# Attention's product with the values in float32, four token tiles at a time

## The chip, the cores and the metric

The kernel runs on one core of a Trainium2 chip. The metric is the device time of one execution in microseconds (us); lower is better. Engine names are those of the profile: PE is TensorE's matrix multiply, PEld its weight load, DVE is VectorE, ACT is ScalarE, POOL is GpSimd, SP is SyncE, which issues the DMAs.

## The reference

One encoder layer on a sequence of 1024 tokens with 1024 channels, all in float32: half a SwiGLU step, a mixing step, half a SwiGLU step, a last RMSNorm. The mixing step projects the normed tokens once and runs two groups of eight heads, latent attention and retention; their outputs are joined and go through one output projection. The change lies in the attention group:

```python
s = (jnp.einsum('bqhd,bkhd->bhqk', qn, k_nope).astype(jnp.float32)
     + jnp.einsum('bqhr,bkr->bhqk', qp, k_pe).astype(jnp.float32))
p = jax.nn.softmax(s * MLA_SCALE, axis=-1)
return jnp.einsum('bhqk,bkhd->bqhd', p.astype(v.dtype), v)
```

There are 8 heads, 1024 queries, 1024 keys, and 64 columns of values to a head. The last line is the product that the change rewrites.

## The kernel before

The program keeps the token sequence as eight tiles of 128 tokens. Its matrix products run on operands of type FP32R (the form that the profile prints as fp32r when it is written; as a matmul operand it prints f32). Where the accuracy needs it, a float32 matrix is kept as two FP32R parts: a rounded copy, made by ACT, and the remainder, which DVE or POOL makes by subtraction. The helper `split` (lines 68 to 83, ACT at L75, subtraction at L79) does this. The helper `mm3` (L118 to L120) multiplies two such pairs with three matmuls.

The layer runs in stages: first feed-forward step, projection, retention, preparation of attention (`mla_prepare`), attention (`attention`), output projection (`out_project`), second feed-forward step, last norm.

In `mla_prepare`, the function `values(t)` forms the values of a token tile with `mm3` into the PSUM tile `dn`, and splits them into the tile `vhl`: for each token tile and head 64 columns of rounded values followed by 64 columns of remainders. A head's slice of `vhl` is thus a stationary operand of 128 keys by 128 columns.

`attention` walks over the 64 pairs of head h and token tile t, in the order h, then t. Step i issues the following:

- `scores(h, t)`: six matmuls of 512 columns (L118 to L120) into the PSUM tile `mm`, a minimum over the row on DVE (`mx`, L1486), and the exponential on ACT (`pr`, L1490), with the row sum as a side result.
- `queries` of the next head at t = 1, eight transposes; `keys2` or `keys` of another head pair at t = 3.
- `flip` of the tile before (i - 1): eight PE transposes of `pr` (L1503) in two halves, each evacuated by `split` into the tile `pT`, as rounded part (ACT) and remainder (DVE). A `pT` tile holds two token tiles, that is 256 query columns, in two parts.
- `values(h, u)` for the pair of token tiles that ended at i - 2: for each of the eight key tiles two matmuls (L1516), the rounded and the remainder part of `pT` against the same `vhl` slice. The result has 128 partitions: the product with the rounded values above, that with the remainders below. ACT copies it to SBUF (`ota`, L1519).
- `finish(h, u)` at i - 4: two transposes of that result (L1526), a DVE reduction that adds the two halves (`ona`, L1528), the reciprocal of the row sums (`ri`, L1531), and a multiplication on POOL (L1532) into the tile that the output projection reads.

The code's order is a priority and not a fixed sequence: the framework that compiles the kernel orders each engine's instructions ahead of time, the earlier-issued first, but lets a later one pass where it reckons that the earlier one's inputs aren't there yet. The PSUM tiles `mm`, `tp` and `dn` have two buffers each. Near the end of the loop, five calls of `next(after)` start parts of the output projection.

Retention, a stage earlier, has its own product with values in two versions. Even heads use two FP32R parts (L1174), with 128 stationary columns. Odd heads use plain float32 with 64 stationary columns:

```python
if whole(h):
    t = (half * 2 + c) * R2 + r
    nc.tensor.matmul(u[0:HD, c * C:(c + 1) * C],
                     self.rv[:, t, h * HD:(h + 1) * HD], shl[:, 1 - r],
```

The line L1167 that the profile names is this call; it has 256 moving columns. It is issued 32 times in the program (four odd heads, two halves, two chunks, two row tiles). Retention's `states` (L1090) is float32 too, with 64 stationary and 128 moving columns; a call issues 16 products, eight that write the lower 64 PSUM partitions and then eight that write the upper 64.

Of the kernel before, what the change touches and what calls it, by code (L numbers as in the profile page):

```python
# [12 lines left out]
F32 = mybir.dt.float32  # L13
F32R = mybir.dt.float32r
# [3 lines left out]
ALU = mybir.AluOpType  # L18
# [3 lines left out]
P = 128  # L22
S = 1024
NT = S // P
# [37 lines left out]
class Layer:  # L62
# [1281 lines left out]
    def mla_prepare(self, raw, w_uq, w_ukv):  # L1344


        nc, v, c = self.nc, self.nc.vector, self.c
        NQ = HA * QH
        raws = [raw[:, i * S:(i + 1) * S] for i in range(3)]
        nc.sync.dma_start(out=raws[0], in_=w_ukv[0])  # L1350
        for j in range(2):
            nc.sync.dma_start(out=raws[1 + j][:, 0:NQ], in_=w_uq[0][j * P:(j + 1) * P, :])
        qpool, pool = yield

        def heads(t):
            return t.rearrange("p (h d) -> p h d", h=HA)

        def transposes(col, tiles, rows=P):
            ps = self.ps.tile([P, 512], F32, name="tp")
            for j, (t, k) in enumerate(tiles):  # L1360
                nc.tensor.transpose(ps[0:rows, j * P:(j + 1) * P],
                                    c[:, t, col + k * P:col + k * P + rows], self.ident)
            return ps

        cqTs = {}

        def cq(u):
            ps = transposes(0, [(2 * u + i, j) for i in range(2) for j in range(2)])
            cqTs[u] = qpool.tile([P, 2, 2, 2, P], F32R, name="cqT")
            dst = cqTs[u].rearrange("p s i j n -> p s (i j n)")  # L1370
            self.split(ps, dst[:, 0], dst[:, 1])

        wv = pool.tile([P, 2, HA * HD], F32R, name="wv", bufs=1)
        wq = qpool.tile([P, 2, 2, NQ], F32R, name="wq", bufs=1)
        again = pool.tile([P, S], F32, name="rawm", bufs=1)
        nc.sync.dma_start(out=again, in_=w_ukv[0])
        cq(0)
        for j in range(2):
            self.split(raws[1 + j][:, 0:NQ], wq[:, 0, j], wq[:, 1, j])
        cq(1)  # L1380
        self.split(raws[0].rearrange("p (h s d) -> p h s d", h=HA, s=2)[:, :, 1],
                   heads(wv[:, 0]), heads(wv[:, 1]))
        keep, vpool = yield
        self.ckvT = keep.tile([P, 2, S], F32R, name="ckvT")
        self.wk = keep.tile([P, 2, HA * HD], F32R, name="wk")
        self.kT = [keep.tile([P, 2, S], F32R, name=f"kT{i}") for i in range(2)]
        self.vhl = vpool.tile([P, NT, HA, 2, HD], F32R, name="vhl")

        def ckv(half):
            ps = transposes(QL, [(half * 4 + j, 0) for j in range(4)])  # L1390
            hs = slice(half * 512, (half + 1) * 512)
            self.split(ps, self.ckvT[:, 0, hs], self.ckvT[:, 1, hs])

        def kpe(half):
            ps = transposes(NC0 - QH, [(half * 4 + j, 0) for j in range(4)], QH)
            hs, pe = slice(half * 512, (half + 1) * 512), slice(HD, QH)
            for kt in self.kT:
                self.split(ps[pe], kt[pe, 0, hs], kt[pe, 1, hs], scale=-SCALE)

        def queries(t):  # L1400
            cqT = cqTs[t // 2]
            q_ps = self.ps.tile([P, S], F32, name="mm")[:, 32:32 + NQ]
            for ns in (slice(0, 5 * QH), slice(5 * QH, NQ)):
                for j in range(2):
                    self.mm3(q_ps[:, ns], (cqT[:, 0, t % 2, j], cqT[:, 1, t % 2, j]),
                             (wq[:, 0, j, ns], wq[:, 1, j, ns]), j == 0, j == 1)
            src, dst = heads(q_ps), self.qn[:, t]
            nc.scalar.activation(out=dst[:, :, 0:HD], in_=src[:, :, 0:HD], func=AF.Copy,
                                 scale=-SCALE)
            self.rope(pool, src[:, :, HD:QH], dst[:, :, HD:QH],  # L1410
                      self.cos[:, t, ::2], self.sin[:, t, ::2], HA, RD // 2)

        def values(t):
            ts_ = slice(t * P, (t + 1) * P)
            v_ps = self.ps.tile([P, 512], F32, name="dn")
            self.mm3(v_ps, (self.ckvT[:, 0, ts_], self.ckvT[:, 1, ts_]),
                     (wv[:, 0], wv[:, 1]), True, True)
            self.split(heads(v_ps), self.vhl[:, t, :, 0], self.vhl[:, t, :, 1])

        ckv(0)  # L1420
        queries(0)
        ckv(1)
        queries(1)
        cq(2)
        self.split(again.rearrange("p (h s d) -> p h s d", h=HA, s=2)[:, :, 0],
                   heads(self.wk[:, 0]), heads(self.wk[:, 1]))
        for t in range(2, NT + 2):
            values(t - 2)
            if t < NT:
                queries(t)  # L1430
            if t == 3:
                cq(3)
            if t in (4, 5):
                kpe(t - 4)

    def attention(self, small, pool, after):
# [35 lines left out]
                hs = slice(half * 512, (half + 1) * 512)  # L1472
                self.split(ps[0:QH], qT[0:QH, 0, hs], qT[0:QH, 1, hs])

        sums, pts = {}, {}

        def scores(h, t):
            kT, qT = self.kT[h % 2], qTs[h]
            ts_ = slice(t * P, (t + 1) * P)
            ps = self.ps.tile([P, S], F32, name="mm")  # L1480
            for n in range(2):
                ns = slice(n * 512, (n + 1) * 512)
                self.mm3(ps[:, ns], (qT[0:QH, 0, ts_], qT[0:QH, 1, ts_]),
                         (kT[0:QH, 0, ns], kT[0:QH, 1, ns]), True, True)
            mx = small.tile([P, 1], F32, name="mx", bufs=4)
            v.tensor_reduce(out=mx, in_=ps, axis=AX.X, op=ALU.min)  # L1486
            pr = pool.tile([P, S], F32, name="pr")
            if t % 2 == 0:
                sums[h, t // 2] = small.tile([P, 2], F32, name="sum", bufs=6)
            nc.scalar.activation(out=pr, in_=ps, func=AF.Exp, scale=-1.0, bias=mx,  # L1490
                                 accum_out=sums[h, t // 2][:, t % 2:t % 2 + 1])
            pts[h, t] = pr

        def flip(h, t):
            pr = pts.pop((h, t))
            if t % 2 == 0:
                pts[h, "T", t // 2] = pool.tile([P, 2, NT, 2 * P], F32R, name="pT")
            pT = pts[h, "T", t // 2]
            for half in range(2):
                ps = self.ps.tile([P, 512], F32, name="tp")  # L1500
                for j in range(4):
                    kt = half * 4 + j
                    nc.tensor.transpose(ps[:, j * P:(j + 1) * P], pr[:, kt * P:(kt + 1) * P],  # L1503
                                        self.ident)
                k4, qs = slice(half * 4, half * 4 + 4), slice(t % 2 * P, (t % 2 + 1) * P)
                self.split(ps.rearrange("p (j q) -> p j q", j=4), pT[:, 0, k4, qs],
                           pT[:, 1, k4, qs])

        def values(h, u):
            pT = pts.pop((h, "T", u))  # L1510
            ps = self.ps.tile([P, 512], F32, name="dn")
            o = ps[:, 0:2 * P]
            for kt in range(NT):
                vl = self.vhl[:, kt, h].rearrange("p s d -> p (s d)")
                for x in range(2):
                    nc.tensor.matmul(o, vl, pT[:, x, kt], start=(kt == 0 and x == 0),  # L1516
                                     stop=(kt == NT - 1 and x == 1))
            ot = small.tile([P, 2 * P], F32, name="ota")
            nc.scalar.copy(out=ot, in_=o)  # L1519
            pts[h, "O", u] = ot  # L1520

        def finish(h, u):
            ot = pts.pop((h, "O", u))
            ps = self.ps.tile([P, 512], F32, name="dn")
            for j in range(2):
                nc.tensor.transpose(ps[:, j * P:(j + 1) * P], ot[:, j * P:(j + 1) * P], self.ident)  # L1526
            on = small.tile([P, 2, HD], F32, name="ona", bufs=1)
            v.tensor_reduce(out=on, in_=ps[:, 0:2 * P].rearrange("p (j s e) -> p j e s", j=2, s=2),  # L1528
                            axis=AX.X, op=ALU.add)
            ri = small.tile([P, 2], F32, name="ri", bufs=6)  # L1530
            v.reciprocal(out=ri, in_=sums.pop((h, u)))  # L1531
            nc.gpsimd.tensor_tensor(out=mixed[:, 2 * u:2 * u + 2, h // 2, h % 2 * HD:(h % 2 + 1) * HD], in0=on,  # L1532
                                    in1=ri.unsqueeze(2).broadcast_to([P, 2, HD]), op=ALU.mult)

        seq = [(h, t) for h in range(HA) for t in range(NT)]
        for i in range(len(seq) + 6):
# [13 lines left out]
                        keys(h // 2 + 1)  # L1550
            if 0 <= i - 1 < len(seq):
                flip(*seq[i - 1])
            for lag, fn in ((2, values), (4, finish)):
                if 0 <= i - lag < len(seq) and seq[i - lag][1] % 2 == 1:
                    fn(seq[i - lag][0], seq[i - lag][1] // 2)
            if i - len(seq) in (-6, -5, -4, -3, 0):
                next(after)

# [127 lines left out]
```

## Time and profile before

| | |
|---|---|
| median of 3 runs | 2060.51 us (2058.77 to 2062.7) |
| profiled execution, time | 2055.27 us |
| profiled execution, span of the core | 2053.1 us |
| mean granted TensorE clock | 0.993 |
| PE busy | 1978.5 us (96%), 10776 records |
| PEld busy | 1699.0 us (83%) |
| DVE busy | 1323.3 us (64%) |
| ACT busy | 818.6 us (40%) |
| POOL busy | 697.4 us (34%) |

A busy time is the union of an engine's records. PE's records overlap each other, since matmuls are pipelined and their ends are modelled; what a matmul costs on PE is therefore read from the distance between the starts of neighbouring records, and not from a record's length.

### The profile page before, as it was taken

The numbers are of one execution on the slowest core, as the hardware profiler recorded it, in microseconds if no ns is written. First come the engines' busy times: TensorE is split into PE (matmuls) and PEld (weight loads), VectorE is DVE, ScalarE is ACT, GpSimd is POOL, SyncE is SP. The second block draws the span as 40 slices with busy tenths as digits, with TensorE's granted clock in tenths as the row PEclk, the third lists the DMA queues.
The fourth block names the chain that finished last, engine by engine and source line by source line (L and its number), as shares of the span: only waits on it lengthen the run. The fifth ranks groups of instructions, "written<-read, shape, count | busy, mean of one in ns | idle before, by whom it ended". The sixth has DMA issues, their size and how long they took to land. (4 is left out here: it accounts for less than half of the span.)

```text
span 2053.1 us, 28597 instructions
## 1 busy us (share of the span) xinstructions
PE 1978.5 (96%) x10776; PEld 1699.0 (83%) x10776; DVE 1323.3 (64%) x2032; ACT 818.6 (40%) x1422; POOL 697.4 (34%) x614
## 2 busy tenths in 40 slices
PE   6999999989999999999999999999999999989998
PEld 5778888877888899998788888997788888868876
DVE  7766666655756644427878887458666566555566
ACT  5322232223444322236567776234222322324444
POOL 0255756754310013213521110000456666553112
PEclk9999999999999999999999999999999999999999
DMA  5244445457866111100100000141354454568773
GB/s 174 67 134 167 141 164 168 142 174 272 282 214 212 42 52 42 53 22 1 57 1 1 1 1 22 42 154 47 108 176 141 156 174 144 174 221 328 226 234 113
DMA packets 209338, 258.86 MB, mean 126 GB/s; under 512 B 14128, under 2 KB 126000, under 8 KB 209200
## 3 DMA queue, kind: packets, MB, share of 16 engines
q1 hardware_dynamic: 208048, 254.93, 37.4%
q8 instruction: 85, 1.39, 0.3%
q10 hardware_dynamic: 1152, 2.10, 0.3%
q14 instruction: 53, 0.43, 0.1%
HBM read 185.15 MB, written 71.83 MB: 125 GB/s over the span
## 5 line engine op out<-in xcount | busy, mean ns | idle before, releaser
L290 PE MATMUL mm<-xt,gu 128*128 128x512 f32 x1584 | 384.8, 392 | 3.3 <-DVE h L322 2.9
L290 PEld LDWEIGHTS mm<-xt,gu 128*128 128x128 f32 x1584 | 298.3, 189 | 66.2 <-ACT h L319 3.7
L79 DVE TENSOR_TENSOR gu<-s,gu 128x512 fp32r<-128x512 f32 x176 | 204.2, 1167 | 140.4 <-ACT gu L75 140.1
L79 DVE TENSOR_TENSOR wd<-rawd,wd 128x1024 fp32r<-128x1024 f32 x143 | 193.8, 1361 | 136.6 <-ACT wd L75 135.7
L290 PE MATMUL dn<-x,gu 128*128 128x512 f32 x1056 | 258.3, 392 | 1.4 <-ACT x L75 1.4
L290 PEld LDWEIGHTS dn<-x,gu 128*128 128x128 f32 x1056 | 197.3, 188 | 42.7 <-ACT x L75 2.0
L75 ACT CAST wd<-rawd 128x1024 fp32r<-128x1024 f32 x143 | 150.4, 1052 | 205.4 <-DMA rawd<-wdt 69.0
L270 POOL TENSOR_TENSOR s<-raw 128x512 f32<-128x512 f32 x40 | 53.8, 1346 | 466.9 <-DMA raw<-in_ffn_w_up 381.9
L619 PE MATMUL mm<-wd 128*128 128x512 f32 x792 | 183.0, 391 | 2.2 <-DVE wd L79 2.0
L619 PEld LDWEIGHTS mm<-wd 128*128 128x128 f32 x792 | 147.9, 188 | 36.3 <-DVE wd L79 5.7
L75 ACT CAST gu<-s 128x512 fp32r<-128x512 f32 x176 | 104.2, 618 | 164.2 <-POOL s L271 154.6
L79 DVE TENSOR_TENSOR gu<-raw,gu 128x512 fp32r<-128x512 f32 x132 | 117.5, 891 | 72.3 <-ACT gu L75 68.8
L322 DVE TENSOR_TENSOR h<-mm,h 128x512 f32<-128x512 f32 x176 | 120.8, 686 | 66.9 <-PE mm L290 66.1
L619 PE MATMUL dn<-wd 128*128 128x512 f32 x462 | 134.2, 396 | 17.6 <-ACT wd L75 13.4
L352 ACT ACTIVATE h<-h 128x512 f32<-128x512 f32 x44 | 27.8, 632 | 286.5 <-DVE h L322 286.5
L290 PE MATMUL tp<-xt,gu 128*128 128x512 f32 x528 | 128.7, 391 | 6.2 <-ACT gu L75 3.3
L619 PE MATMUL tp<-wd 128*128 128x512 f32 x462 | 130.7, 390 | 0.0
L290 PE MATMUL mm<-x,gu 128*128 128x512 f32 x528 | 127.3, 390 | 0.0
L290 PEld LDWEIGHTS tp<-xt,gu 128*128 128x128 f32 x528 | 98.4, 188 | 29.7 <-ACT gu L75 4.6
L619 PEld LDWEIGHTS dn<-wd 128*128 128x128 f32 x462 | 86.6, 189 | 39.6 <-ACT wd L75 14.3
L290 PEld LDWEIGHTS mm<-x,gu 128*128 128x128 f32 x528 | 98.8, 188 | 21.4 <-DVE h L322 0.6
L75 ACT CAST gu<-raw 128x512 fp32r<-128x512 f32 x132 | 81.1, 618 | 59.6 <-DMA raw<-in_ffn_w_gate 58.8
(356 smaller groups left out, 3881.7 us busy)
## 6 DMA issues: line engine op xcount, KB each, us to landing
hid<-h SPq DMA_DIRECT2D x154, 256.0 KB, 3.3
rawd<-hid SPq DMA_DIRECT2D x154, 256.0 KB, 3.3
raw<-in_ffn_w_gate SPq DMA_DIRECT2D x52, 512.0 KB, 4.2
raw<-in_ffn_w_up SPq DMA_DIRECT2D x44, 512.0 KB, 5.9
rawd<-wdt SPq DMA_DIRECT2D x88, 256.0 KB, 3.8
early<-in_ffn_w_down SPq DMA_DIRECT2D x40, 512.0 KB, 5.5
wdt<-early SPq DMA_DIRECT2D x80, 256.0 KB, 2.2
rawd<-in_ffn_w_down SPq DMA_DIRECT2D x66, 256.0 KB, 3.6
```

Of the source, the lines that this page charges most:

```text
L75: a = nc.scalar.copy(out=hi, in_=src)
L79: b = eng.tensor_tensor(out=lo, in0=src, in1=hi.bitcast(F32), op=ALU.subtract)
L270: tt(out=s[1], in0=u[:, h1], in1=u[:, h2], op=ALU.add)
L290: nc.tensor.matmul(out, l[:, p], r[:, q], start=start and dt == 0 and i == 0, stop=dt == 3 and i == 2, skip_group_check=True)
L322: v.tensor_tensor(out=out, in0=ps, in1=other, op=ALU.add)
L352: nc.scalar.activation(out=g, in_=g, func=AF.Silu)
L619: nc.tensor.matmul(out, w[:, p, 0, ts_], w[:, q, 1], start=start and i == 0, stop=stop and i == 2, skip_group_check=True)
```

## The change

The values stay whole: `v` is one float32 tile with 64 columns a head, written by one ACT copy, and no remainders are formed. `flip` copies the transposed probabilities whole too, one half by ACT and the other by DVE. A `pT` tile now holds four token tiles (512 query columns) in one float32 part. `values` runs one float32 matmul per key tile, 64 stationary and 512 moving columns, into the lower 64 partitions; it is issued in two parts of four matmuls, at i - 2 and i - 3. `finish` transposes four blocks of 64 partitions and multiplies straight out of PSUM on DVE; the reduction and the POOL multiplication are gone.

```diff
-        self.vhl = vpool.tile([P, NT, HA, 2, HD], F32R, name="vhl")
+        self.v = vpool.tile([P, NT, HA * HD], F32, name="v")
...
-            self.split(heads(v_ps), self.vhl[:, t, :, 0], self.vhl[:, t, :, 1])
+            nc.scalar.copy(out=self.v[:, t], in_=v_ps)
...
-        sums, pts = {}, {}
+        sums, pts, G = {}, {}, 4
...
-                pts[h, "T", t // 2] = pool.tile([P, 2, NT, 2 * P], F32R, name="pT")
+                pts[h, "T", t // G] = pool.tile([P, NT, G * P], F32, name="pT")
...
-                k4, qs = slice(half * 4, half * 4 + 4), slice(t % 2 * P, (t % 2 + 1) * P)
-                self.split(ps.rearrange("p (j q) -> p j q", j=4), pT[:, 0, k4, qs],
-                           pT[:, 1, k4, qs])
-
-        def values(h, u):
-            pT = pts.pop((h, "T", u))
-            ps = self.ps.tile([P, 512], F32, name="dn")
-            o = ps[:, 0:2 * P]
-            for kt in range(NT):
-                vl = self.vhl[:, kt, h].rearrange("p s d -> p (s d)")
-                for x in range(2):
-                    nc.tensor.matmul(o, vl, pT[:, x, kt], start=(kt == 0 and x == 0),
-                                     stop=(kt == NT - 1 and x == 1))
-            ot = small.tile([P, 2 * P], F32, name="ota")
-            nc.scalar.copy(out=ot, in_=o)
+                dst = pT[:, half * 4:half * 4 + 4, t % G * P:(t % G + 1) * P]
+                src = ps.rearrange("p (j q) -> p j q", j=4)
+                if half:
+                    v.tensor_copy(out=dst, in_=src)
+                else:
+                    nc.scalar.copy(out=dst, in_=src)
+
+        def values(h, u, part):
+
+            if part == 0:
+                pts[h, "V", u] = self.ps.tile([P, G * P], F32, name="dn")
+            pT, o = pts[h, "T", u], pts[h, "V", u][0:HD]
+            for kt in range(part * NT // 2, (part + 1) * NT // 2):
+                nc.tensor.matmul(o, self.v[:, kt, h * HD:(h + 1) * HD], pT[:, kt],
+                                 start=kt == 0, stop=kt == NT - 1)
+            if part == 0:
+                return
+            del pts[h, "T", u], pts[h, "V", u]
+            ot = small.tile([P, G * P], F32, name="ota")
+            nc.scalar.copy(out=ot[0:HD], in_=o)
             pts[h, "O", u] = ot
...
-            for j in range(2):
-                nc.tensor.transpose(ps[:, j * P:(j + 1) * P], ot[:, j * P:(j + 1) * P], self.ident)
-            on = small.tile([P, 2, HD], F32, name="ona", bufs=1)
-            v.tensor_reduce(out=on, in_=ps[:, 0:2 * P].rearrange("p (j s e) -> p j e s", j=2, s=2),
-                            axis=AX.X, op=ALU.add)
-            ri = small.tile([P, 2], F32, name="ri", bufs=6)
+            for j in range(G):
+                nc.tensor.transpose(ps[:, j * HD:(j + 1) * HD], ot[0:HD, j * P:(j + 1) * P],
+                                    self.ident[0:HD, 0:HD])
+            ri = small.tile([P, G], F32, name="ri", bufs=6)
             v.reciprocal(out=ri, in_=sums.pop((h, u)))
-            nc.gpsimd.tensor_tensor(out=mixed[:, 2 * u:2 * u + 2, h // 2, h % 2 * HD:(h % 2 + 1) * HD], in0=on,
-                                    in1=ri.unsqueeze(2).broadcast_to([P, 2, HD]), op=ALU.mult)
+            v.tensor_tensor(out=mixed[:, G * u:G * (u + 1), h // 2, h % 2 * HD:(h % 2 + 1) * HD],
+                            in0=ps[:, 0:G * HD].rearrange("p (j e) -> p j e", j=G),
+                            in1=ri.unsqueeze(2).broadcast_to([P, G, HD]), op=ALU.mult)
...
-            for lag, fn in ((2, values), (4, finish)):
-                if 0 <= i - lag < len(seq) and seq[i - lag][1] % 2 == 1:
-                    fn(seq[i - lag][0], seq[i - lag][1] // 2)
+            for lag, fn, args in ((2, values, (0,)), (3, values, (1,)), (4, finish, ())):
+                if 0 <= i - lag < len(seq) and seq[i - lag][1] % G == G - 1:
+                    fn(seq[i - lag][0], seq[i - lag][1] // G, *args)
```

## Rows read from the trace of the kernel before

**Rows 1.** Windows of the attention stage: each engine's busy us (instructions), granted clock, DMA share.

```profile
1050.00:1100.00 50.00, 49.88 (x325) 44.02 (x324) 39.58 (x58) 35.84 (x70) 2.79 (x6) 0.97 0.00 1
1100.00:1150.00 50.00, 49.85 (x340) 44.41 (x339) 41.24 (x62) 36.93 (x72) 4.54 (x9) 1.00 0.01 1
...
sum 228.00, PE 226.96 PEld 201.75 DVE 184.49 ACT 165.94 POOL 20.94; mean PE 45.39 PEld 40.35 DVE 36.90 ACT 33.19 POOL 4.19
```

**Rows 2.** Timeline of PE in attention: start, us, engine, line, operation, tiles, shapes, count.

```profile
1113.02 1.09 PE L1503 MATMUL tp<-ident,pr 128*128 128x128 f32 x8
1113.87 1.67 PE L1516 MATMUL dn<-pT,vhl 128*128 128x256 f32 x12
1115.38 0.38 PE L1526 MATMUL dn<-ident,ota 128*128 128x128 f32 x2
1115.52 0.48 PE L118 MATMUL mm<-kT,qTa 96*128 96x512 f32 x1
...
1116.99 1.04 PE L1503 MATMUL tp<-ident,pr 128*128 128x128 f32 x8
1117.78 0.47 PE L118 MATMUL mm<-kT,qTa 96*128 96x512 f32 x1
...
1119.25 0.64 PE L1516 MATMUL dn<-pT,vhl 128*128 128x256 f32 x4
1119.86 1.09 PE L1503 MATMUL tp<-ident,pr 128*128 128x128 f32 x8
...
1126.70 1.09 PE L1503 MATMUL tp<-ident,pr 128*128 128x128 f32 x8
```

**Rows 3.** Timeline of all engines, the chain of one tile's probabilities.

```profile
1117.19 1.22 DVE L1486 TENSOR_REDUCE mx<-mm 128x1 f32<-128x1024 f32 x1 [0.83 <-PE mm L120]
...
1118.59 1.13 ACT L1490 ACTIVATE pr<-mm,mx 128x1024 f32<-128x1024 f32 x1
...
1119.86 0.86 PEld L1503 LDWEIGHTS tp<-ident,pr 128*128 128x128 f32 x8 [0.18 <-ACT pr L1490]
```

**Rows 4.** Groups by form, attention stage: busy us, mean ns, idle before and its releaser.

```profile
L79 DVE TENSOR_TENSOR pT<-tp,pT 128x512 fp32r<-128x512 f32 x128 | 83.1, 684 | 15.0 <-ACT pT L75 15.0
...
L1516 PE MATMUL dn<-pT,vhl 128*128 128x256 f32 x512 | 76.2, 290 | 0.6 <-ACT pT L75 0.2
...
L75 ACT CAST pT<-tp 128x512 fp32r<-128x512 f32 x128 | 69.9, 589 | 57.4 <-PE tp L1503 56.4
...
L1528 DVE TENSOR_REDUCE ona<-dn 128x128 f32<-128x256 f32 x32 | 13.5, 421 | 6.5 <-PE dn L1526 5.7
...
L1519 ACT COPY ota<-dn 128x256 f32<-128x256 f32 x32 | 12.2, 380 | 1.4 <-PE dn L1516 1.4
```

**Rows 5.** Retention's float32 product, the line's own view: ns min/median/max.

```profile
L1167 PEld LDWEIGHTS dn<-x,rv x64: 132/137/137, 935.9 to 1012.0; 128*64 128x64 f32 x64
L1167 PE MATMUL dn<-x,rv x64: 379/379/430, 935.9 to 1012.3; 128*64 128x256 f32 x64
```

**Rows 6.** Timeline of PE around two float32 blocks in retention.

```profile
947.52 0.60 PE L1014 MATMUL tp<-ident,rk 128*128 128x128 f32 x4
948.05 1.94 PE L1167 MATMUL dn<-x,rv 128*64 128x256 f32 x8
949.92 0.38 PE L118 MATMUL mm<-x 128*128 128x256 f32 x1
...
957.79 1.94 PE L1167 MATMUL dn<-x,rv 128*64 128x256 f32 x8
959.57 0.60 PE L1090 MATMUL tp<-x,rk 128*64 128x128 f32 x4
```

**Rows 7.** Timeline of PE over retention's `states`, both partition halves.

```profile
959.57 3.28 PE L1090 MATMUL tp<-x,rk 128*64 128x128 f32 x32
962.78 0.39 PE L118 MATMUL mm<-x 128*128 128x256 f32 x1
```

**Rows 8.** The same call in the line's own view: ns min/median/max.

```profile
L1090 PE MATMUL tp<-x,rk x32: 272/272/323, 959.6 to 962.6; 128*64 128x128 f32 x32
```

**Rows 9.** Waits between 1000 and 1050 us: engine, line, what it waited for, us, times, longest.

```profile
PE dn L118 <- DVE vhl L79: 1.4, 1, 1.4
```

More of the change, by code (lines that the diff above doesn't have):

```diff
@@ L1487, in scores @@
             pr = pool.tile([P, S], F32, name="pr")
-            if t % 2 == 0:
-                sums[h, t // 2] = small.tile([P, 2], F32, name="sum", bufs=6)
+            if t % G == 0:
+                sums[h, t // G] = small.tile([P, G], F32, name="sum", bufs=6)
             nc.scalar.activation(out=pr, in_=ps, func=AF.Exp, scale=-1.0, bias=mx,
-                                 accum_out=sums[h, t // 2][:, t % 2:t % 2 + 1])
+                                 accum_out=sums[h, t // G][:, t % G:t % G + 1])
             pts[h, t] = pr
@@ L1495, in flip @@
             pr = pts.pop((h, t))
-            if t % 2 == 0:
-                pts[h, "T", t // 2] = pool.tile([P, 2, NT, 2 * P], F32R, name="pT")
-            pT = pts[h, "T", t // 2]
+            if t % G == 0:
+                pts[h, "T", t // G] = pool.tile([P, NT, G * P], F32, name="pT")
+            pT = pts[h, "T", t // G]
             for half in range(2):
```

## The prediction

> **What bounds the kernel now.** I read the page's busy shares first (PE 96%), and then the windows of the stage that the change touches, since a share over the whole span says nothing of one stage. In attention, PE is busy for 226.96 of 228 us, DVE for 184.49, ACT for 165.94 and POOL for 20.94 [rows 1]. Busy PE alone proves little, because its records overlap; so I went to the timeline, to see whether PE's starts follow each other without holes. They do. From the flip at 1113.02 to the flip at 1126.70 four token tiles pass in 13.68 us, 6.84 for a pair [rows 2], and the pair is made up of PE work alone: two flips (0.85 and 0.79), two sets of scores (1.47 each), the product with the values in two pieces (12 matmuls from 1113.87 to 1115.38 = 1.51, and 4 from 1119.25 to 1119.86 = 0.61), and two transposes of finish (0.14). The reader is to see that the only hole is inside the 0.61: four matmuls at 0.12 each take 0.48, and the flip behind them waited the rest for the exponential (0.18 by the weight load's row) [rows 3]. So PE is the bound of this stage, and what the change does to PE is what it does to the time. The pulled-forward piece of four also shows what fills such holes: the product with the values is the only work that may come early.
>
> **The product itself.** Before: 2.12 us for a pair of token tiles (1.51 + 0.61), 4.24 for four, and there are 16 groups of four (8 heads, two each), 67.8 us in all. That is 512 matmuls [rows 4].
>
> After: eight float32 products for a group, 128 in all. What is one worth? Retention has float32 products with the same 64 stationary columns and 128 partitions, and 256 moving columns. The code issues 32 of them, the trace has 64 records [rows 5]: a float32 product is two records, each with its weight load. Eight records last from 957.79 to 959.57, when a block of the same form follows: 1.78 us [rows 6]. The first record of a block can be 0.05 longer (430 against 379 ns) [rows 5], so a record comes every (1.78 - 0.05) / 8 = 0.216 us. With 128 moving columns, four records span 0.60, the last of them lasting 0.27 [rows 6, 8]: (0.60 - 0.27) / 3 = 0.11. Doubling the columns adds 0.107, so at 512 columns I expect 0.216 + 2 x 0.107 = 0.43. Sixteen records make 6.88 us for a group.
>
> The trace has another price to read there. The form with 64 stationary columns is entered and left with a gap. Four transposes at 0.109 should take 0.44, but the float32 block starts 0.53 after them (947.52 to 948.05); the same eight records take 1.87 when a 128-column form follows (948.05 to 949.92) and 1.78 when it doesn't [rows 6]. With the first record's 0.05 that is 0.09 + 0.05 + 0.09 = 0.23 for a block. Between the 128-column forms of attention I see no such gap: eight flips and the change to values take 0.85, no more than 8 x 0.109 [rows 2]. How many blocks will a group make? The two parts of `values` are issued a step apart, with a flip and scores between them, so two; and where a flip waits for its exponential, a product will be pulled forward as the four matmuls are now, which cuts the first part in two. I take three blocks: 0.70 for a group; two would be 0.46, five 1.15, none 0.
>
> So the group goes from 4.24 to 6.88 + 0.70 = 7.58, and 16 x 3.34 = **+53.4 us**.
>
> **Holes that open.** From the last score matmul's slot (1116.99) to its flip (1119.86) 2.87 us pass: the minimum (1.22), the exponential (1.13) and the hand-overs [rows 2, 3]. PE fills them with the flip before (0.79) and the next scores (1.47); 0.61 must come from elsewhere. In the new order, per four tiles, two flips have a part of `values` ahead of them (some 3.5 us each). The flip of a group's first tile can have a product pulled forward, or the eight transposes of `queries`. The flip of the last tile has only finish, four transposes, up to 0.44: 0.17 is left, 16 x 0.17 = **+2.7** (bounds 0, and 16 x 0.61 = 9.8).
>
> **Finish.** Four transposes of 128 columns for a group now (0.14 to 0.22 a pair), four of 64 partitions and 64 moving columns after. The trace has no such form. Bounds: half the price, -0.22 for a group, and the old price with one 0.19 entry and exit; -3.5 and +3.0 in all. I take **0**, since the weight load of 128 columns stays. The DVE reduction, the reciprocal count and the POOL multiplication change off the path.
>
> **DVE and ACT.** DVE loses 128 subtractions of 684 ns (87.6 us) and 32 reductions (13.5), and gets 64 copies, at most 684 each (43.8), and 16 multiplications, at most 684 each (11) [rows 4]: some 138 us left. ACT loses 64 of 128 casts of 589 (37.7); 16 copies of twice the size replace 32 of 380 ns (from 12.2 to at most 12.2): some 128 left. All of this relief is costed at nothing: PE's unbroken starts hide both engines now [rows 1, 2], and will hide them better when PE's work grows. If that cover were gone, the minimum would be what a queue on DVE delays, and the hole above would grow by the length of one copy.
>
> **Preparation.** Eight subtractions leave DVE. One of them held a PSUM buffer so that PE waited 1.4 us [rows 9]; ACT's copy stays, so I take **-1.4** (bounds 0 and -2.8, the same wait twice). `v` is 16 KB a partition smaller than `vhl`, which moves the pools that are opened after it; no row shows a wait on such memory, so 0. The change issues no DMA and moves none past another.
>
> **The sum** is 53.4 + 2.7 - 1.4 = +54.7, made against the profiled execution (2055.27, of which 2053.1 is span), which gives 2110. That execution lies 5.2 below the median of the runs shown; against the median the sum gives 2060.5 + 54.7 = **2115.2 us**.
>
> **The rivals.** *The float32 records overlap.* This is the one that ends not slower. In `states` 16 records write the lower 64 partitions, then 16 the upper; the 32 take 3.21 us up to the next form, where 32 x 0.109 + 0.09 would be 3.58 [rows 7]. About 0.37 is saved, so records of 64 columns do run at once to some extent where the two halves meet. If the new ones paired up like that, 16 records would take 3.44, the group 4.14, 16 x -0.10 = -1.6, and with +2.7 and -1.4 the time would be 2060.2; it decides from a record distance of 0.21 down. Against it: all new products write partitions 0 to 63, as retention's do, and those follow each other at the full 0.216 [rows 6].
>
> The Trainium skill, page TensorEngine Tiling (Array Packing), sections Tiling Modes and Performance Considerations, says that operands of at most 64 columns let the array run as two independent tiles, up to twice as fast, each tied to its own PSUM partitions. The overlap at the border [rows 7] agrees with it; read as a plain factor of two it would give this rival's time, read with its tie to partitions it gives none here.
>
> *No gaps, no holes.* The switches are hidden, or the parts lie in fewer blocks, and finish fills the last hole: 16 x (6.88 - 4.24) - 1.4 = +40.8, 2101. For it: longer records leave more time to load weights, 137 ns in 430 [rows 5]. Against it: they were visible with 216 [rows 6].
>
> *The flips lose their cover.* The compiled order leaves the products in one piece in each group, and three more flips of each group wait 0.61: 16 x 1.83 = +29, 2144. For it: the order was worked out ahead of time from reckoned durations, and the pieces are coarser, 0.86 each. Against it: today's order fills every hole but 0.13.
>
> *The relief counts.* If the stage were held by DVE's or ACT's chain, PE would show holes; it shows 0.13 in 6.84 [rows 2], 16 x 0.26 = 4 us at most, which the first term already takes in; no chance of its own.
>
> **How the numbers follow.** Overlap 3%, no gaps 18%, lost cover 7%, my sum 72%. The range: from 2100, where no switch costs anything, to 2132, which takes five blocks a group (+7.2), full holes at the last flip (+7.1) and the dearer finish (+3); the overlap and the full loss of cover lie outside. A measurement of this kernel can tell about 0.2% (4 us) from no change. Faster 1%, same 2%, slower 97%.
>
> **What would show it.** In the profile after: 256 records of form 128*64 by 128x512, at distances of 0.43; gaps of about 0.1 where that form begins and ends; four tiles without `queries` in 13.68 + 3.34 + 0.17 = 17.2 us; PE still busy throughout, DVE near 138 us and ACT near 128 in the stage; no wait of `dn` L118 on a subtraction in preparation. I am wrong if a record comes at 0.22, if `states` and the new products behave alike, or if PE shows holes before more than one flip in four.

## The result and the profile after

The changed kernel takes 2117.86 us (median of 4 runs, 2116.5 to 2120.51), and the kernel before takes 2059.64 (2058.42 to 2062.7) in the runs beside it. The ratio is 1.0282, with a 95% interval of 1.0264 to 1.03: slower, by 58.2 us.

The page gives the span and the busy time of each engine:

```profile
span 2115.0 us, 27863 instructions
PE 2042.0 (97%) x10520; PEld 1664.9 (79%) x10520; DVE 1270.7 (60%) x1928; ACT 791.1 (37%) x1342; POOL 681.0 (32%) x582
```

PE has 256 fewer instructions and is busy for 63.5 us more. DVE, ACT and POOL are all less busy than before. So work went from three engines to the one that bounds the kernel. The windows of the attention stage, read as [rows 1], show the same in one stage:

```profile
1100.00:1150.00 50.00, 50.00 (x223) 29.09 (x222) 22.59 (x30) 23.38 (x41) 2.52 (x2) 1.00 0.00 1
...
sum 291.00, PE 288.72 PEld 168.60 DVE 140.28 ACT 142.49 POOL 9.00; mean PE 48.12 PEld 28.10 DVE 23.38 ACT 23.75 POOL 1.50
```

PE is still busy throughout, at the full granted clock (1.00). DVE fell from 41 us in 50 to 23, and that gave nothing back.

How long is the stage? I measure it from the last matmul of L1149, which ends retention, to the first of the output projection. The lines' own views give the first and last start of each. First the kernel before, then the one after:

```profile
L1149 PE MATMUL dn<-x,x x72: 278/283/387, 934.2 to 1006.4; 128*128 128x256 f32 x72
L118 PE MATMUL mm<-kT,qTa x128: 389/397/628, 1043.3 to 1268.1; 96*128 96x512 f32 x128
L118 PE MATMUL dn<-ckvT,m x112: 281/281/364, 1282.2 to 1351.7; 128*128 128x256 f32 x112
```

```profile
L1149 PE MATMUL dn<-x,x x72: 278/283/386, 938.4 to 1010.7; 128*128 128x256 f32 x72
L118 PE MATMUL mm<-kT,qTa x128: 388/398/504, 1046.3 to 1326.9; 96*128 96x512 f32 x128
L118 PE MATMUL dn<-ckvT,m x112: 276/281/367, 1345.2 to 1414.1; 128*128 128x256 f32 x112
```

Before, it is 1282.2 - 1006.4 = 275.8 us; after, 1345.2 - 1010.7 = 334.5. The difference, 58.7, holds the loss of 58.2 between the medians. (The spans of the two profiled executions differ by 61.9: the one after also ended retention 4.3 us later, a start that lies between 1005.9 and 1010.7 over all runs here, and of which I make nothing.) In two parts: from retention to the first scores 36.9 became 35.6 (-1.3), and from there to the output projection 238.9 became 298.9 (+60.0).

PE's timeline shows where inside (four token tiles without `queries`, to be read against [rows 2]):

```profile
1131.54 1.04 PE L1503 MATMUL tp<-ident,pr 128*128 128x128 f32 x8
1132.34 0.49 PE L118 MATMUL mm<-kT,qTa 96*128 96x512 f32 x1
...
1133.91 1.07 PE L1518 MATMUL dn<-pT,v 128*64 128x512 f32 x2
1134.92 1.09 PE L1503 MATMUL tp<-ident,pr 128*128 128x128 f32 x8
1135.94 2.79 PE L1518 MATMUL dn<-pT,v 128*64 128x512 f32 x6
1138.66 0.50 PE L118 MATMUL mm<-kT,qTa 96*128 96x512 f32 x1
...
1140.15 1.04 PE L1503 MATMUL tp<-ident,pr 128*128 128x128 f32 x8
1141.12 3.65 PE L1518 MATMUL dn<-pT,v 128*64 128x512 f32 x8
1144.69 0.50 PE L118 MATMUL mm<-kT,qTa 96*128 96x512 f32 x1
...
1146.19 1.04 PE L1503 MATMUL tp<-ident,pr 128*128 128x128 f32 x8
1147.15 0.46 PE L1531 MATMUL dn<-ident,ota 64*128 64x64 f32 x4
1147.54 0.50 PE L118 MATMUL mm<-kT,qTa 96*128 96x512 f32 x1
...
1149.04 0.71 PE L1503 MATMUL tp<-ident,pr 128*128 128x128 f32 x5
```

The cycle went from 13.68 to 1149.04 - 1131.54 = 17.50 us. The product stands in three pieces of 2, 6 and 8 records, 1.01 + 2.72 + 3.57 = 7.30, where it took 4.24. The reader should also compare the four flips, which are the same eight transposes each time. The one ahead of scores takes 0.80. Those ahead of the product take 0.97 and 1.02, and the one ahead of `finish` takes 0.96. The switch to the 64-wide float32 form is paid there, 0.10 of the 0.17; the other 0.07 is taken up below, under The product. No bracket with an idle time stands at any row: PE has no wait here that the view lists.

### The profile page after: what moved, and what is told of

Same layout as the page of the kernel before. It is cut to its first block, busy times and chain, and to the rows that moved or that the text cites. A ratio compares the mean times of both kernels' runs of the same rounds, so it can differ in the third digit from the quotient of the medians.

```text
span 2115.0 us, 27863 instructions
## 1 busy us (share of the span) xinstructions
PE 2042.0 (97%) x10520; PEld 1664.9 (79%) x10520; DVE 1270.7 (60%) x1928; ACT 791.1 (37%) x1342; POOL 681.0 (32%) x582
## 4 chain that ended last, share of the span: by engine, by line
PE 34%; DMA 6%; DVE 5%; POOL 2%; ACT 2%; issue 1%; SPq 1%; ACTq 0%; POOLq 0%; DVEq 0%
PE mm L290 8%; PE dn L1518 6%; PE dn L290 4%; PE tp L1503 3%; DMA rawd<-wdt 2%; PE tp L290 2%; PE mm L118 2%; DMA rawd<-in_ffn_w_down 2%; PE dn L118 1%; PE dn L120 1%; PE dn L119 1%; DMA raw<-in_ffn_w_up 1%; PE mm L119 1%; PE mm L120 1%; DVE wd L79 1%
## 5 line engine op out<-in xcount | busy, mean ns | idle before, releaser
L270 POOL TENSOR_TENSOR s<-raw 128x512 f32<-128x512 f32 x40 | 53.4, 1336 | 551.9 <-DMA raw<-in_ffn_w_up 537.7
L1486 DVE TENSOR_REDUCE mx<-mm 128x1 f32<-128x1024 f32 x64 | 78.2, 1223 | 118.3 <-PE mm L120 116.7
L1518 PE MATMUL dn<-pT,v 128*64 128x512 f32 x256 | 119.9, 602 | 0.0
```

The costliest lines, as they stand in the source:

```text
L270: tt(out=s[1], in0=u[:, h1], in1=u[:, h2], op=ALU.add)
L1518: nc.tensor.matmul(o, self.v[:, kt, h * HD:(h + 1) * HD], pT[:, kt], start=kt == 0, stop=kt == NT - 1)
```

## The experiments

The times of the two kernels and of the nine runs, each against runs of the kernel before on the same chip, and the length of the stage as defined above, from the one profiled execution of each:

| run | median us | ratio, 95% interval | stage us |
|---|---|---|---|
| before | 2059.64 | 1 | 275.8 |
| after | 2117.86 | 1.0282 [1.0264, 1.03] | 334.5 |
| after_again | 2116.06 | 1.0269 [1.0244, 1.0294] | 334.6 |
| two_tiles | 2119.75 | 1.0277 [1.0254, 1.0299] | 340.9 |
| wide_product | 2101.35 | 1.0189 [1.0164, 1.0214] | 321.1 |
| wide | 2100.16 | 1.0185 [1.0159, 1.0212] | 319.5 |
| halves | 2076.26 | 1.0068 [1.0045, 1.0091] | 292.9 |
| halves_first | 2061.15 | 1.0005 [0.9992, 1.0019] | 275.3 |
| no_remainder | 2057.94 | 0.9989 [0.9976, 1.0003] | 276.5 |
| values_whole | 2026.69 | 0.9838 [0.9816, 0.9861] | 244.7 |
| rounded | 2023.75 | 0.982 [0.9796, 0.9844] | 242.4 |

**wide: the same float32 records, without the 64-wide form.** The stationary operand takes the values of two neighbouring heads, 128 columns, and `finish` transposes whole blocks; the other head's half is not used.

```diff
...
-                nc.tensor.matmul(o, self.v[:, kt, h * HD:(h + 1) * HD], pT[:, kt],
+                nc.tensor.matmul(o, self.v[:, kt, h // 2 * P:(h // 2 + 1) * P], pT[:, kt],
...
-            nc.scalar.copy(out=ot[0:HD], in_=o)
+            nc.scalar.copy(out=ot, in_=o)
...
-                nc.tensor.transpose(ps[:, j * HD:(j + 1) * HD], ot[0:HD, j * P:(j + 1) * P],
-                                    self.ident[0:HD, 0:HD])
+                nc.tensor.transpose(ps[:, j * P:(j + 1) * P], ot[:, j * P:(j + 1) * P], self.ident)
...
```

> The changed kernel with 128 stationary columns in the float32 product (both heads of a pair, of whose results one is used) and whole 128-partition transposes in finish, so that attention has no form of 64 columns or 64 partitions left. Theory (the float32 records cost 0.43 us each whatever the width, and each of three blocks a group pays 0.23 for the change of form, finish some 0.28): records stay at 0.43, the gaps go, 16 x (0.70 + 0.28) = 16 us, from 2117.9 to 2102. Rival (the gaps belong to float32 and not to the form): 2118 as the changed kernel, or slower, since a weight load has 128 columns now.

Measured: 2100.16 us, where the rival had 2118, and a stage 15.0 us shorter than after's. PE's timeline of this run:

```profile
1115.21 1.04 PE L1503 MATMUL tp<-ident,pr 128*128 128x128 f32 x8
1116.08 3.60 PE L1518 MATMUL dn<-pT,v 128*128 128x512 f32 x8
1119.12 0.80 PE L118 MATMUL mm<-kT,qTa 96*128 96x512 f32 x1
1119.76 0.40 PE L119 MATMUL mm<-kT,qTa 96*128 96x512 f32 x1
...
1120.91 1.04 PE L1503 MATMUL tp<-ident,pr 128*128 128x128 f32 x8
...
1123.37 0.39 PE L120 MATMUL mm<-kT,qTa 96*128 96x512 f32 x1
1123.69 1.09 PE L1503 MATMUL tp<-ident,pr 128*128 128x128 f32 x8
```

The flip ahead of the product takes 0.87 here and 0.97 in after. Eight records and the scores behind them take 1120.91 - 1116.08 = 4.83, and in after 1146.19 - 1141.12 = 5.07. They have to be taken together: the first score record starts early, 3.04 after the product began, but the next one starts 0.64 later (1119.12 to 1119.76), where the pace of scores is 0.23. The sum, 4.83, is what eight records at 0.43 and six at 0.23 make. Such a piece thus costs some 0.3 us more in the 64-wide form, and three pieces some 0.9 a group; the stage's 15.0 is 0.94 a group. Twice the stationary columns cost nothing: the records' number and pace set the product's price.

**wide_product: only the product wide.** `finish` keeps the form of the change, 64 partitions by 64 columns, and takes its head's half.

```diff
...
+            rows = slice(h % 2 * HD, (h % 2 + 1) * HD)
...
+                nc.tensor.transpose(ps[:, j * HD:(j + 1) * HD], ot[rows, j * P:(j + 1) * P],
+                                    self.ident[rows, rows])
```

> As the wide kernel, but finish transposes blocks of 64 partitions, as the changed kernel does. Theory: the product's gaps go (11 us), finish's stay: 2117.9 - 11 = 2107, some 4.5 above the wide kernel. Rival (finish costs nothing, as I had predicted): 2102, the same as the wide kernel.

Measured: 2101.35 us, which medians can't tell from wide; the stage is 1.6 us longer. The rival of this run was nearer: of the 15.0 us that wide gains, the product has 13.4, and `finish` 1.6. The 1.6 is net: in eleven of its sixteen groups wide has a small hole behind `finish` (see Holes below), which the switch of `finish` fills in this run.

**two_tiles: groups of two tiles, 256 columns.** G is 2, so that there are twice as many records of half the length.

```diff
-        sums, pts, G = {}, {}, 4
+        sums, pts, G = {}, {}, 2
...
-                pts[h, "V", u] = self.ps.tile([P, G * P], F32, name="dn")
+                pts[h, "V", u] = self.ps.tile([P, 512], F32, name="dn")[:, 0:G * P]
```

> The changed kernel with two token tiles and 256 columns at a time in place of four and 512. Theory (what a record costs goes with its columns, 0.216 for 256, and what a block costs doesn't): the records take the same 6.9 us for four tiles, but there are about twice as many blocks and twice as many finishes: 16 x (0.70 + 0.28) more, 2134. Rival (gaps are hidden or belong to the long records): 2118, no change.

Measured: 2119.75 us; the expected extra was not there, and the median is the one that the rival (2118) gave. The trace counts 71 pieces of the product where I had reckoned with about 96; after has 47. And 31 of the 32 pieces of `finish` now lie directly against a piece of the product, so that both share one visit to the 64-wide forms: PE makes 72 visits, where after makes 63. The stage is 6.4 us longer. Nine visits at 0.3 would be some 2.7 of it; the rest was not taken apart. So this run neither proves the price of a switch nor speaks against it: how many switches there are, the compiled order decides, and I had guessed that number.

**halves: alternate key tiles write the lower and the upper 64 partitions.** This tests the rival that records overlap where the halves meet. The two halves are added after `finish`'s transposes.

```diff
-                nc.tensor.matmul(o, self.v[:, kt, h * HD:(h + 1) * HD], pT[:, kt],
-                                 start=kt == 0, stop=kt == NT - 1)
+                rows = slice(kt % 2 * HD, (kt % 2 + 1) * HD)
+                nc.tensor.matmul(o[rows], self.v[:, kt, h * HD:(h + 1) * HD], pT[:, kt],
+                                 start=kt < 2, stop=kt >= NT - 2, skip_group_check=True)
...
```

> The changed kernel, with the even key tiles summed in the lower 64 PSUM partitions and the odd ones in the upper 64, whole transposes and a reduction that adds the two in finish. Theory (records of 64 columns that write different halves run at once, the order within a block of n products gives (n + 1) x 0.43): with blocks of 3, 1 and 4 a group takes 4.7 + 0.70 in place of 7.30 + 0.24, finish loses 0.28: some 35 us less, 2083; if they pair up without loss, 2063. Rival (float32 records never overlap here): finish alone gains, 2113.

Measured: 2076.26 us, between the two times of the theory (2083 and 2063) and far from the rival's 2113. The timeline of this run:

```profile
1121.19 1.07 PE L1519 MATMUL dn<-pT,v 128*64 128x512 f32 x2
1122.19 1.09 PE L1503 MATMUL tp<-ident,pr 128*128 128x128 f32 x8
1123.21 1.93 PE L1519 MATMUL dn<-pT,v 128*64 128x512 f32 x6
1125.07 0.50 PE L118 MATMUL mm<-kT,qTa 96*128 96x512 f32 x1
...
1126.57 1.04 PE L1503 MATMUL tp<-ident,pr 128*128 128x128 f32 x8
1127.54 1.94 PE L1519 MATMUL dn<-pT,v 128*64 128x512 f32 x8
1129.40 0.50 PE L118 MATMUL mm<-kT,qTa 96*128 96x512 f32 x1
```

Eight records take 1.86 us in place of 3.57. Six take 1.86 as well, and two (one product alone) take 1.00, no less than in after. So two neighbouring products that write different halves run at once, and one without a partner pays the full price. A group takes 1.00 + 1.86 + 1.86 = 4.72 in place of 7.30, and 16 x 2.58 = 41.3 is near the stage's gain (41.6). The piece of one product that the order pulls forward breaks a pair in each group.

The Trainium skill, page TensorEngine Tiling (Array Packing), section Tiling Modes, says that narrow operands work as tiles that run independently, each tied to its own PSUM partitions, and that a change of the mode drains the engine. The pairs of this run agree with the first (1.86 against 3.57), and the gaps of after with the second, though only for float32, as the run rounded shows.

**halves_first: keep the pairs together.** As halves, and the first half of the product is issued ahead of the flip, not behind it.

```diff
+            if 0 <= i - 2 < len(seq) and seq[i - 2][1] % G == G - 1:
+                values(seq[i - 2][0], seq[i - 2][1] // G, 0)
...
-            for lag, fn, args in ((2, values, (0,)), (3, values, (1,)), (4, finish, ())):
+            for lag, fn, args in ((3, values, (1,)), (4, finish, ())):
```

> The halves kernel with the first part of the product issued ahead of the flip of its step, so that its four products lie in one piece. Theory (records that write different halves start in pairs, 6 ns apart, but only within a piece: four products take 1.72, three as long, one 0.86; each piece pays 0.14 and an entry): a group's product goes from 4.73 to 3.74, and one entry of 0.09 goes: 16 us less than the halves kernel, 2060, no different from the kernel before. Rival (the order of pieces doesn't count, the pairing has reached its limit): 2076.

Measured: 2061.15 us, level with before. The timeline:

```profile
1115.68 1.94 PE L1519 MATMUL dn<-pT,v 128*64 128x512 f32 x8
1117.55 1.09 PE L1503 MATMUL tp<-ident,pr 128*128 128x128 f32 x8
...
1120.84 1.94 PE L1519 MATMUL dn<-pT,v 128*64 128x512 f32 x8
1122.70 0.50 PE L118 MATMUL mm<-kT,qTa 96*128 96x512 f32 x1
```

Two pieces of four products at 1.87 and 1.86 make 3.73 a group, 0.99 less than halves, and with one switch fewer the stage is 17.6 us shorter. Float32 values at the price of the two-part form are to be had, but they need both halves of the partitions.

**no_remainder: is DVE's relief worth anything?** This is the kernel before without the 128 subtractions of `flip`. The product takes the rounded part of the probabilities twice, in place of the remainder, so PE's work stays.

```diff
-                self.split(ps.rearrange("p (j q) -> p j q", j=4), pT[:, 0, k4, qs],
-                           pT[:, 1, k4, qs])
+                nc.scalar.copy(out=pT[:, 0, k4, qs], in_=ps.rearrange("p (j q) -> p j q", j=4))
...
-                    nc.tensor.matmul(o, vl, pT[:, x, kt], start=(kt == 0 and x == 0),
+                    nc.tensor.matmul(o, vl, pT[:, 0, kt], start=(kt == 0 and x == 0),
```

> The kernel before, without the 128 DVE subtractions in flip; the product runs as often as before, with the rounded part of the probabilities taken twice, so their remainder is left out. Theory (PE holds the stage, relief of DVE is worth nothing but the 0.13 us wait of a flip): 2059.6 less 0 to 4. Rival (DVE's queue delays the minimum, and so the flips): 10 us or more faster.

Measured: 0.9989 [0.9976, 1.0003]. The windows' sum over the 228 us of [rows 1]:

```profile
sum 228.00, PE 226.88 PEld 201.53 DVE 107.92 ACT 167.38 POOL 20.43; mean PE 226.88 PEld 201.53 DVE 107.92 ACT 167.38 POOL 20.43
```

DVE went from 184.49 to 107.92 us and PE from 226.96 to 226.88: 76.6 us taken off an engine that is not the bound, for nothing that can be measured.

**rounded: the change, with FP32R operands.** The shape, the 64 columns and the order of issue stay; `v` and `pT` are written as FP32R, and the remainders of both are left out.

```diff
-        self.v = vpool.tile([P, NT, HA * HD], F32, name="v")
+        self.v = vpool.tile([P, NT, HA * HD], F32R, name="v")
...
-                pts[h, "T", t // G] = pool.tile([P, NT, G * P], F32, name="pT")
+                pts[h, "T", t // G] = pool.tile([P, NT, G * P], F32R, name="pT")
```

> The changed kernel with its two new tiles, the values and the probabilities, in FP32R in place of float32: same shapes, same order of work, but the remainders of both operands are left out of the product. Theory (the time is the float32 records' on PE): 128 records at 0.23 in place of 256 at 0.43, a group loses 4.9 to 5.1 us, less the holes that open before flips with so little product left to fill them (0.61 each, one or two a group): 2118 - 80 + 8 to 16, so 2045 to 2055. Rival (four tiles at a time and the changes of form are what costs): 2090 or more.

Measured: 2023.75 us, over 20 us faster than expected. The timeline:

```profile
1121.23 1.04 PE L1503 MATMUL tp<-ident,pr 128*128 128x128 f32 x8
1122.02 1.17 PE L1518 MATMUL dn<-pT,v 128*64 128x512 f32 x4
1123.03 0.39 PE L118 MATMUL mm<-kT,qTa 96*128 96x512 f32 x1
1123.26 0.40 PE L119 MATMUL mm<-kT,qTa 96*128 96x512 f32 x1
```

Two things that I expected are missing. The flip ahead of the product takes 0.79, as ahead of scores, and the scores behind it keep their pace (0.23): the 64-wide form has no gap when its operands are FP32R. And the holes hardly opened, although a product is now one record (four in 1.01 us) where it was two of 0.43: PE's list of waits has one flip in the stage, 1.4 us at the last tile, and by the starts seven more flips past the start of attention are late, by 0.3 us at most and 0.7 in all. The page FP8 and Floating Point Precision of the Trainium skill, section TensorE Precision Notes, says that true float32 takes four passes through the array; 0.86 against 0.25 us a product agrees roughly.

**values_whole: the remainder of the probabilities alone left out.** Groups of four tiles as in the change, the 128 columns of `vhl` as before, and one matmul per key tile in place of two. The evacuation copies `pT` as in the change, and `finish` keeps its reduction. The central edit, set against the kernel before:

```diff
...
-                for x in range(2):
-                    nc.tensor.matmul(o, vl, pT[:, x, kt], start=(kt == 0 and x == 0),
-                                     stop=(kt == NT - 1 and x == 1))
+                for x in range(1):
+                    nc.tensor.matmul(o, vl, pT[:, x, kt], start=(kt == 0 and x == 0),
+                                     stop=(kt == NT - 1 and x == 0))
...
```

> The kernel before, four token tiles and 512 columns at a time, with the probabilities rounded to FP32R and their remainder left out of the product; the values keep both parts, 128 stationary columns. Theory (FP32R's record of 512 columns is worth 0.23 whatever the width of the stationary operand, and no FP32R form pays for being entered): as the rounded kernel, which has 64 columns, 2024, and 2 less for finish without a form of 64 partitions. Rival (twice the width costs weight-load time, or the 64-column kernel gained by pairing): 10 us or more above the rounded kernel.

Measured: 2026.69 us. The form 128*128 by 128x512 takes 1.01 us for four, like the 64-wide one in rounded, so for FP32R the width costs nothing either. Both runs beat both kernels, by leaving out remainders that the kernel before keeps. The change itself, unaltered, was run once more with this one:

> The changed kernel once more, beside the next two on their chip. 1.028 times the kernel before, as measured first.

Measured: 2116.06 us, a ratio of 1.0269, which holds the first result, and a stage of 334.6.

## Why the prediction was right

The mechanism and the size held: 2115.2 us was forecast, in a range from 2100 to 2132, and 2117.86 came; of the stage, +54.7 was forecast and +58.7 found. Term by term, with the measured cost of a group read from the cycle above and taken 16 times:

| term | forecast | found |
|---|---|---|
| product with its switches | +53.4 | 16 x 3.50 = +56.0 |
| `finish` | 0 | 16 x 0.28 = +4.5 |
| holes ahead of flips | +2.7 | 0 in the cycle, +1.0 once at the end |
| preparation | -1.4 | -1.3 |
| start of attention | not seen | -2.9 |
| rest of the cycle | 0 | +0.6 |
| sum | +54.7 | +57.9 (stage: +58.7) |

That the sum came so near is in part luck. The product, `finish` and the rest of the cycle were forecast 7.7 us too low, the holes and the start of attention 4.6 too high.

**The product.** A record every 0.429 us, two for a product, three pieces a group: all three as forecast. The pieces take 7.30, and the entries another 0.17 behind each of two flips (0.97 against 0.80) and 0.10 behind the scores (1.57 against 1.47), 7.74 in all; less 4.24 that is 3.50, where I had 3.34. What was off is less the switch than the price of the old product, of which I took off too much. I had measured a switch by the transposes ahead of a float32 block against 0.109 each, which makes 0.87 for eight. Ahead of FP32R, eight take 0.80 by the starts, since the first FP32R record starts early; it is then the longer to the next, so that no time is gained. The twelve matmuls behind the flip of [rows 2] take 1.51, where twelve at 0.12 make 1.44. That 0.07 belonged to the flip and stood in my 4.24 twice; when the form behind becomes float32, it stands in the flip again, as wide's 0.87 shows by itself.

**The attribution of the gap.** I wrote that the form with 64 stationary columns is entered and left with a gap. Rounded has the form and no gap; wide has float32 with 128 columns and no gap either, only the 0.07 in the flip. It takes both, float32 and 64 columns. For this change the two can't be told apart and the number held; for the run rounded my expectation, built on that sentence, missed.

**Finish.** Costed at 0, with +3.0 as the upper bound; the cycle shows four transposes at 0.39 and 0.17 more in the flip ahead, 0.56, against 2 x 0.14: +4.5, above my bound. The bound had the switch in it (0.19); what it lacked is the same 0.07, since the 0.14 of the old pairs also ends at an early start. The groups by form show that the transposes are cheaper by themselves:

```profile
L1531 PE MATMUL dn<-ident,ota 64*128 64x64 f32 x64 | 7.3, 235 | 0.2
```

In the trace their starts are 0.063 us apart where a 128-column one takes 0.109; the visit to the form costs more than that saves, though part of it fills a hole, as follows.

**Holes.** In the cycle none, but the need for them was there. The flip of a group's last tile (1149.04) has the flip ahead, `finish` and one set of scores to cover its exponential: 1149.04 - 1146.19 = 2.85 us. In wide the same stretch takes 1123.69 - 1120.91 = 2.78, and there the flip waits: it starts 0.05 us after its exponential's end, and 0.32 after the last score record, where the pace is 0.23. Eleven of wide's groups have this hole of 0.09; I had priced 0.17. In the changed kernel the switch of `finish` fills it. I had added up two terms that cover each other. One hole is left where nothing comes after, at the last tile:

```profile
1328.58 0.46 PE L1531 MATMUL dn<-ident,ota 64*128 64x64 f32 x4
1330.38 1.09 PE L1503 MATMUL tp<-ident,pr 128*128 128x128 f32 x8 [1.35 <-ACT pr L1490]
```

From the end of `finish`'s 0.39 to that flip 1.4 us pass. Before, the same flip waited some 0.4, since twelve matmuls of a product (1.51 us) ran ahead of it; hence +1.0.

**Relief.** DVE was forecast at 138 us in the stage and found at 140.28. ACT was forecast at 128 and found at 142.49. I had taken lengths of single casts off a busy time, in which records overlap: ACT's groups add up to 185.6 us in the windows before, of which 165.94 is busy, and to 152.7 and 142.49 after. Neither mattered; no_remainder shows the relief of DVE alone to be worth nothing. The waits of the stage say why: both engines wait for PE.

```profile
DVE mx L1486 <- PE mm L120: 116.4, 43, 4.2
ACT pT L1510 <- PE tp L1503: 85.6, 47, 3.8
...
PE tp L1503 <- ACT pr L1490: 1.3, 1, 1.3
```

**Preparation.** The wait of [rows 9] is gone, and the stretch from retention to the first scores is 1.3 shorter. A wait of the weight load for the new copy of `v`, 1.4 us in the same list, stands elsewhere; the balance holds both.

**Start of attention.** This term was in the rows of before and I had not taken it in. PE stands still for 1.79 us there, waiting for the first exponential, and then runs at the lower of its two clock levels. The kernel before, timeline of PE and windows of 1 us:

```profile
1048.92 1.09 PE L1503 MATMUL tp<-ident,pr 128*128 128x128 f32 x8 [1.79 <-ACT pr L1490]
1049.77 0.48 PE L118 MATMUL mm<-kT,qTa 96*128 96x512 f32 x1
...
1051.75 0.63 PE L120 MATMUL mm<-kT,qTa 96*128 96x512 f32 x1
1052.18 0.63 PE L118 MATMUL mm<-kT,qTa 96*128 96x512 f32 x1
1052.60 1.49 PE L1503 MATMUL tp<-ident,pr 128*128 128x128 f32 x8
1053.85 0.48 PE L119 MATMUL mm<-kT,qTa 96*128 96x512 f32 x1
```

```profile
1051.00:1052.00 1.00, 1.00 (x4) 0.81 (x3) 0.76 (x2) 0.00 (x0) 0.00 (x0) 0.50 0.00 0
```

Score matmuls are 0.43 apart there instead of 0.23, at a granted clock of 0.50 (1.2 GHz). Seven score records stand between the two flips and take 2.83 us, where a set of six and one more take 1.47 + 0.23 = 1.70; the second flip takes 1.25 against 0.79. Together that is 1.6 us. After, the order of the first tiles differs, PE stands still for 0.53, and the clock stays at 1.00:

```profile
1049.00:1053.00 4.00, 3.47 (x23) 2.70 (x21) 2.83 (x4) 3.49 (x7) 2.45 (x2) 1.00 0.00 0
```

That is 1.3 + 1.6 = 2.9 us gained. values_whole has the low stretch again (0.66 in the same window) and rounded doesn't (1.00). Over all eleven profiles, the three kernels that split the values in preparation (before, no_remainder, values_whole) have it, and the eight that copy them whole don't. Which order of the first tiles brings it was not tested apart.

**The rivals.** No gaps and no holes (2101) is near what wide measures, 2100.16, with the gaps taken away: the rival's arithmetic was right and its condition wasn't met. The overlap (2060.2) is what halves_first measures, 2061.15: it exists, but not when all products write partitions 0 to 63. The flips did not lose their cover. Of the 0.8 us of the stage that no term holds, nothing is known; the groups that contain `queries` were not taken apart.

## What to carry to other kernels

When PE has no holes, price an operand type by records times their pace, read from a block of the same type elsewhere in the trace, and price the switches separately by what stands ahead of a block and behind it; relief of the other engines was worth nothing here (no_remainder). Float32 with 512 moving columns costs two records, 0.43 us apart, where FP32R costs one, 0.23 apart; with 64 stationary columns it gets half of that back only if neighbouring products write different halves of the PSUM partitions, without another form between the partners. Before a product is made more exact or its remainders are kept, look at which of the parts cost a record: here leaving out one remainder, with groups of four tiles, is worth some 33 us (values_whole).

## What the runs showed of the hardware that was not expected

- A float32 product of 64 stationary columns pays where its form begins and ends: the flip ahead of it takes 0.97 us, against 0.87 ahead of one of 128 columns, and eight records with the scores behind them 5.07 against 4.83. In FP32R 64 columns pay nothing (flip ahead 0.79, as ahead of scores).
- Starts mislead where float32 changes to FP32R. The first FP32R record starts early (eight transposes 0.80 against 0.87 ahead of float32) and is the longer to the next (0.64 behind wide's product, where the pace is 0.23); the sum is that of the paces.
- Two float32 products of 64 columns whose results go to different halves of the PSUM partitions run at once (records of a pair start 6 to 7 ns apart in the trace): four products in 1.86 us, three in 1.86, one in 1.00.
- In FP32R four products of 512 columns take 1.01 us with 64 stationary columns and with 128.
- A wait of 1.79 us on PE at the start of attention was followed by some 3 us at half the clock (granted 0.50); one of 0.53 us at the same place was not.
